# The twelve probability-times-value matmuls of a head pair, one after the other

## The chip, the cores and the metric

One core of one Trainium2 chip runs the whole program in one launch. The metric is device time in microseconds (us), from the first instruction to the last, the median of several runs. Engines are called as in the profile: PE is TensorE (matmuls; PEld its weight loads), DVE VectorE, ACT ScalarE, POOL GpSimd, SP the engine that issues most DMAs.

## The reference, cut to what matters

Two layers over 512 latent tokens and 256 context tokens, 1024 wide. Layer 0 mixes tokens by grouped-query attention, layer 1 by latent attention; each has 16 heads of 64. An MLP of 4096 follows each. What the change touches is the last line of the attention:

```python
s = jnp.einsum('bqhgd,bkhd->bhgqk', qi, k) * scale
p = jax.nn.softmax(s, axis=-1)
return jnp.einsum('bhgqk,bkhe->bqhge', p, v)
```

Latent queries see all 768 keys. Context queries (layer 0 only, since layer 1 needs no context output) see the 256 context keys.

## The kernel before, in words

Both attentions run through one class, `Attn`. Its `run` walks over items. An item is one head and 128 latent queries (or, in layer 0, one head and all 256 context queries). A head pair and 256 latent queries, a "half" below, is four items, so each layer has 8 pairs and 16 halves. Layer 0 has eight more, smaller groups for the context.

For an item PE makes the scores into a PSUM tile `big` (two of them): L867 and L868 in layer 0, L858 and L859 for its context queries, L1369, L1372 and L1373 in layer 1. DVE finds the maximum of each row (L713) and ACT the exponentials `prob` (L714). Two items later (`lag`) PE transposes the six blocks of `prob` (L729, into PSUM tiles `one`, of which there are four), and ACT (L736) and DVE (L738) copy them to `pT` in SBUF. When both heads and both query tiles of a half are there, `values` makes the steps that are left:

- `sums_of`: reciprocals of the row sums, and a broadcast of them (`rb`) on ACT
- six `block` steps, one for each 128 keys: two matmuls (L753), one for each head. Each has 64 output columns in the array: the first head's result goes to partitions 0 to 63 of the accumulator, the second head's to 64 to 127. Operands are float32
- `end`: two transposes of the broadcast sums (L762), a copy (L764) and the product that ends the half (L765)

`run` keeps these eight steps in a list `av` and takes two of them in each item, between that item's scores and its transposes. So one half's steps are spread over four items.

The code's order is not yet the order on an engine. When the program is built, a scheduler places the instructions of each engine by its own estimates of when inputs are ready, with buffers as limits. `tc.keep_in_program_order(x)` puts `x` behind the instruction that was recorded just before it on the same engine; the scheduler may still put others between the two. Loads of later weights (`early_weights`, `at`) and, in layer 0, the sums for the modulation vectors on POOL (`fill`: L204, L208, closed on PE by L215) hang on the count of items.

Of the kernel before, what the change touches and what calls it, by code (L numbers as in the profile page):

```python
# [19 lines left out]
P = 128  # L20
D = 1024
# [18 lines left out]
def backbone(ctx, tc, a, out):  # L40
    """Every float32 product runs as three float32r products: an operand is split exactly into
    hi = float32r(x) and lo = x - hi (12 significant bits each), and hi*hi, hi*lo and lo*hi are
    accumulated in PSUM."""
# [77 lines left out]
    def ada_bias(src, n, queue=nc.sync):  # L121
        """Row g of src [4, n] in rows 32 g and 32 g + 1."""
        ring = halves if n == P else brows
        ring.append(ring.pop(0))
        b = ring[-1]
        for g in range(4):
            queue.dma_start(b[32 * g : 32 * g + 2, 0:n], src[g : g + 1, :].to_broadcast([2, n]))
        return b[:, 0:n]
# [10 lines left out]
    def ada_finish(layer, v, half, n, o, bias):  # L139
        """o: PSUM [P, 512], the sums in rows 32 g + stream: to DRAM (gates) or transposed to SBUF."""  # L140
        w = D // n
        q = w // 4
        row = ada_row(o[:, 0:q], bias)
        if v % 3 == 2:
            for g in range(4):
                c0 = half * w + g * q
                nc.sync.dma_start(gates[2 * layer + v // 3, :, c0 : c0 + q], row[32 * g : 32 * g + 2, :])
            return
        tp = o[:, 256 : 256 + q]
        m = q // P  # L150
        for c in range(m):
            nc.tensor.transpose(tp[:, c * P : (c + 1) * P], row[:, c * P : (c + 1) * P], ident)
        if (layer, v) not in modT:
            modT[layer, v] = const.tile([P, KD, 2], F32, name=f"modT{layer}{v}")
        mv = modT[layer, v].rearrange("p (n g j) s -> p n j g s", n=n, g=4)
        for s in range(2):
            nc.vector.tensor_copy(
                out=mv[:, half, :, :, s], in_=tp.rearrange("p (c g r) -> p c g r", c=m, g=4)[:, :, :, s]
            )

    def ada_pe(layer, v, ts, bias):
        """Modulation vector v by TensorE alone: a list of steps."""
        o = []

        def step(k):
            if k == 0:
                o.append(one())
            for g in range(4):
                nc.tensor.matmul(
                    o[0][32 * g : 32 * g + 32, 0:256], scT[:, k, :], ts[k][:, g * 256 : g * 256 + 256],  # L170
                    start=(k == 0), stop=(k == KD - 1),
                )

        steps = [lambda k=k: step(k) for k in range(KD)]
        return steps + [lambda: ada_finish(layer, v, 0, 1, o[0], bias)]

    def ada_vec(layer, v, half, n, streams, pools, mult):
        """Part `half` of n of modulation vector v: silu(c)-weighted rows summed over the contraction
        tiles by GpSimd (or VectorE), over the partitions by TensorE. A list of steps to run; the last
        returns the step that ends it, for later. pools: tiles for the raw rows, the weighted rows and  # L180
        the sums."""
# [41 lines left out]
    class Fill:  # L223
        """Steps of side work; one that returns a further step has it run `lag` calls later."""
# [20 lines left out]
    def mod_ab(layer, sub, ln):  # L245
        """The per-feature scale and shift that take the normalized rows (before LayerNorm's gain
        and bias) to the modulated input of sublayer `sub`."""
        sh, sc = modT[layer, 3 * sub], modT[layer, 3 * sub + 1]
        A = const.tile([P, KD, 2], F32, name=f"modA{layer}{sub}")
        nc.vector.tensor_scalar_add(A, sc, 1.0)  # L250
        B = const.tile([P, KD, 2], F32, name=f"modB{layer}{sub}")
        nc.vector.tensor_tensor(
            out=B, in0=A, in1=lnbT[:, ln, :].unsqueeze(2).to_broadcast([P, KD, 2]), op=ALU.mult
        )
        nc.vector.tensor_tensor(out=B, in0=B, in1=sh, op=ALU.add)
        nc.vector.tensor_tensor(
            out=A, in0=A, in1=lngT[:, ln, :].unsqueeze(2).to_broadcast([P, KD, 2]), op=ALU.mult
        )
        return A, B

    def rsqrt(dst, src, n, scale):
        """dst = (src * scale + EPS) ** -0.5"""
        nc.vector.tensor_scalar(
            out=dst, in0=src, scalar1=scale, scalar2=EPS, op0=ALU.mult, op1=ALU.add
        )
        nc.gpsimd.tensor_tensor(out=dst, in0=dst, in1=nhalf[:, 0:n], op=ALU.pow)
# [7 lines left out]
    class LN:  # L274
        """LayerNorm of row tiles, the residual copy, and the modulated transpose of tile pairs."""
# [22 lines left out]
        def stats(self, z):  # L298
            """[1 / sigma, -mean / sigma] and the mean of the rows."""
# [19 lines left out]
        def gain(self, ln):  # L319
            """LayerNorm's gain and bias rows on every partition."""  # L320
            for nm in ("ln_g", "ln_b"):
                t = self.xp.tile([P, D], F32, name=nm)
                nc.sync.dma_start(t, a[nm][ln : ln + 1, :].to_broadcast([P, D]))
                self.gb[nm] = t
# [6 lines left out]
        def to_act(self, zs, col, s, A, B, aH, aL, temp, dve=(1,), pin=False):  # L331
            """Two normalized row tiles -> columns [col, col + 256) of the split activations; steps
            that return their last instructions."""
# [225 lines left out]
    def norm_a(src, n):  # L559
        """1 / rms of n heads of 64."""  # L560
# [11 lines left out]
    def norm_b(src, ss, n, t, i):  # L572
        """The normalized heads, or (latent tokens) the rotary terms: two summands."""
# [55 lines left out]
    def q_split(q, QS, lo, n):  # L629
        """Token tiles [lo, lo + n) of a head pair's q -> per head, the split transpose on two halves."""  # L630
# [48 lines left out]
    def early_weights(src, ws, n, i0, i1, step, at):  # L679
        """The first n weights of src: loads from item i0 of the attention on, splits from item i1 on."""  # L680
# [15 lines left out]
    class Attn:  # L696
        """Softmax attention over head pairs, in items of one head and 128 or (context) 256 queries.
        Of six transposed blocks ACT evacuates nact, DVE the others."""
# [5 lines left out]
        def softmax(self, S, ntile, width, sm):  # L704
            """S: PSUM [P, 2, 512], scores in [:, :, 0:width]; one row set over both banks, or
            (ntile 2) one in each. The exponentials; their row sums go to sm."""
# [16 lines left out]
        def transposed(self, pt, parts):  # L723
            """parts: (first block, PSUM evacuation to, by ACT or not); blocks of pt, transposed."""
# [15 lines left out]
        def values(self, PT, sums, v, kts, dst):  # L740
            """dst [P, 2, P]: both heads' outputs, transposed, over the row sums; a list of steps."""
# [8 lines left out]
            def block(n, kt):  # L750
                acc = env["acc"]
                for hh in range(2):
                    nc.tensor.matmul(  # L753
                        acc[64 * hh : 64 * hh + 64, 0:256], v(kt, hh), PT[hh][:, :, n, :],
                        start=(n == 0), stop=(n == len(kts) - 1),
                    )

# [12 lines left out]
            return [sums_of] + [lambda n=n, kt=kt: block(n, kt) for n, kt in enumerate(kts)] + [end]  # L770


        def run(self, first, prep, scores, vcol, o_of, npair, ctx_scores, fill, at):
            """first: the state of pair 0; prep(pair) -> (state, steps); scores(state, head, tile, S);
            vcol(kt, head); o_of(pair) -> destination; fill: further steps, one to an item; at: what
            to do at which item."""
# [10 lines left out]
            for i in range(len(items) + lag):  # L787
# [15 lines left out]
                av = av[2:]  # L803
                if i >= lag:
# [13 lines left out]
                    if h == 1 and (hf is None or q == 1):  # L818
# [5 lines left out]
                        )  # L824
                if steps:
                    steps.pop(0)()
# [69 lines left out]
    def out_proj(layer, wsrc, early, tiles, col0, o_of, x_src, x_dst, wxp, aH, aL, A, B, lnst, zst, x_ln):  # L896
        """y = attention output @ w_o, merged and normalized, tile by tile of 128 tokens. The rows
        of x still lack the gain and bias of LayerNorm x_ln, if any. Returns what is left to do for
        the last two tiles."""
# [53 lines left out]
    def mlp(layer, tiles, aH, aL, x_src, late, zst, lnst, fill, before_tail, finish):  # L953
        """Squared-ReLU MLP over the token tiles, G hidden tiles at a time; the last R groups are
        accumulated together, token tile by token tile. The rows of x still lack the gain and bias of
        the sublayer before's LayerNorm."""
# [122 lines left out]
        # With one stream its gate goes into the last weights' columns, else onto their products.  # L1079
# [57 lines left out]
    def low_rank(acc, n, sq, ss, cn, v, gT, dH, dL, col, late):  # L1137
        """RMS norm of a [P, 128 n] row tile; its gain and the split transpose are left to do."""
# [26 lines left out]
    def kv_tile(t):  # L1165
        """The latent rows and the rotary key of a tile."""
# [102 lines left out]
    def rope_keys(lo, n):  # L1269
        """The rotary key of token tiles [lo, lo + n), transposed, into every head's keys."""  # L1270
# [164 lines left out]
def _rope_tables(axis_dim):  # L1435
    """cos and signed sin of the 2-D rotary embedding, [P, 2, NLT, 2 * axis_dim]."""
# [12 lines left out]
def _layout(i):  # L1449
    f = {k: np.asarray(v) for k, v in i.items()}  # L1450

    def units(w, cols, per):
        """[K, *] columns `cols`, `per` contraction tiles side by side in each [P, per * cols]."""
# [63 lines left out]
```

## Time and profile before

| what | value |
|---|---|
| median of three runs | 1727.52 us (1726.24 to 1728.4) |
| span of the profiled execution | 1726.7 us |
| PE busy | 1670.8 us, 97% |
| DVE, ACT, POOL busy | 1125.1, 730.7 and 450.4 us |
| mean granted TensorE clock | 0.989 |
| first attention, first scores to last value matmul | about 137 to 358 us |
| second attention | about 1090 to 1293 us |

The profiled execution has no time of its own beside its span; the median of the three runs is 0.8 us above that span. "Busy" is time with at least one instruction of the engine running. PE's matmuls overlap each other, so an engine that is busy for the whole of a stretch can still do its work faster or slower. What is to be read is the distance from the start of one matmul to the start of the next.

### The profile page before, as it was taken

Reading aid. Unit: us, or ns where it says so; the run is one execution under the profiler, and the core shown is the slowest. Engines: PE = TensorE matmul, PEld = TensorE weight load, DVE = VectorE, ACT = ScalarE, POOL = GpSimd, SP = SyncE. Lnnn points to the kernel's source line nnn. Section 1 sums busy time; section 2 is a strip of 40 time slices with the busy share of each in tenths; the row PEclk is TensorE's granted clock in tenths of the full one; section 3 lists DMA queues with packets and bytes.
Section 4 is the critical chain, followed back from the end, with each engine's and each line's share of the span. In section 5 each row is a group of like instructions: output and inputs, shape, how many; then the busy total and the mean of one; then the engine's idle time right before and its main releaser. Section 6 shows DMA issues by size and latency. Waiting matters only on the chain.

```text
span 1726.7 us, 23376 instructions
## 1 busy us (share of the span) xinstructions
PE 1670.8 (97%) x9054; PEld 1377.1 (80%) x9054; DVE 1125.1 (65%) x1721; ACT 730.7 (42%) x1346; POOL 450.4 (26%) x317
## 2 busy tenths in 40 slices
PE   7998999999999999999999899999999899999996
PEld 5875777678988898889889798877778888888885
DVE  3688767756758676556547776656648745555578
ACT  2324666734544345233212256666654532222221
POOL 0157688300214154324013531000004200000034
PEclk9999999999999999999999999999999999999998
DMA  9412112132445256444212232000003532232222
GB/s 318 130 50 98 50 49 87 50 110 92 144 143 171 84 173 207 136 132 137 80 55 84 70 104 89 1 1 25 25 32 128 195 110 92 92 98 93 91 85 73
DMA packets 56384, 172.03 MB, mean 100 GB/s; under 512 B 7096, under 2 KB 10320, under 8 KB 56272
## 3 DMA queue, kind: packets, MB, share of 16 engines
q1 hardware_dynamic: 56240, 170.51, 29.6%
q8 instruction: 71, 1.16, 0.3%
q14 instruction: 41, 0.34, 0.1%
q10 hardware_dynamic: 32, 0.02, 0.0%
HBM read 161.03 MB, written 9.47 MB: 99 GB/s over the span
## 4 chain that ended last, share of the span: by engine, by line
PE 79%; DVE 11%; DMA 4%; ACT 2%; POOL 2%; issue 1%; SPq 0%; DVEq 0%; ACTq 0%; POOLq 0%
PE one L89 9%; PE one L91 9%; PE one L90 9%; PE one L753 8%; PE big L990 7%; PE big L994 7%; PE big L993 7%; PE one L729 5%; DVE wl L65 2%; PE one L930 2%; PE one L931 2%; PE one L934 2%; POOL xr L208 2%; DMA raw<-in_mlp_w_dram 2%; DMA sraw<-in_w_ada_dram 1%; PE big L1369 1%
## 5 line engine op out<-in xcount | busy, mean ns | idle before, releaser
L62 ACT CAST wh<-raw 128x1024 fp32r<-128x1024 f32 (+3 forms) x169 | 171.4, 1031 | 396.4 <-PE one L91 216.1
L65 DVE TENSOR_TENSOR wl<-raw,wh 128x1024 fp32r<-128x1024 f32 (+3 forms) x169 | 218.4, 1307 | 167.0 <-ACT wh L62 166.5
L990 PE MATMUL big<-actH,wh 128*128 128x384 f32 (+2 forms) x800 | 280.8, 352 | 3.2 <-ACT wh L62 3.2
L994 PE MATMUL big<-actH,wl 128*128 128x384 f32 (+2 forms) x800 | 279.6, 350 | 0.3 <-DVE wl L65 0.3
L993 PE MATMUL big<-actL,wh 128*128 128x384 f32 (+2 forms) x800 | 279.8, 350 | 0.0
L89 PE MATMUL one<-wh,hh 128*128 128x512 f32 x640 | 256.5, 402 | 12.4 <-ACT hh L62 7.3
L90 PE MATMUL one<-wl,hh 128*128 128x512 f32 x640 | 256.2, 400 | 1.3 <-DVE wl L65 1.3
L91 PE MATMUL one<-wh,hl 128*128 128x512 f32 x640 | 254.5, 399 | 2.7 <-DVE hl L65 2.7
L1072 DVE TENSOR_TENSOR yacc<-yacc,one 128x512 f32<-128x512 f32 x260 | 174.4, 683 | 110.7 <-PE one L91 110.1
L208 POOL TENSOR_TENSOR xr<-xr,raw 128x1024 f32<-128x1024 f32 x49 | 131.4, 2681 | 241.6 <-ACT raw L206 226.3
L990 PEld LDWEIGHTS big<-actH,wh 128*128 128x128 f32 x800 | 150.2, 188 | 16.6 <-ACT wh L62 4.1
L994 PEld LDWEIGHTS big<-actH,wl 128*128 128x128 f32 x800 | 150.3, 188 | 13.5 <-DVE wl L65 0.7
L993 PEld LDWEIGHTS big<-actL,wh 128*128 128x128 f32 x800 | 150.3, 188 | 12.3 <-issue 0.4
L89 PEld LDWEIGHTS one<-wh,hh 128*128 128x128 f32 x640 | 122.2, 191 | 43.6 <-ACT hh L62 8.4
L713 DVE TENSOR_REDUCE nm<-big 128x1 f32<-128x768 f32 x128 | 122.1, 954 | 46.7 <-PE big L1373 29.6
L91 PEld LDWEIGHTS one<-wh,hl 128*128 128x128 f32 x640 | 121.7, 190 | 33.0 <-DVE hl L65 4.1
L90 PEld LDWEIGHTS one<-wl,hh 128*128 128x128 f32 x640 | 122.2, 191 | 27.6 <-DVE wl L65 1.7
L328 POOL TENSOR_TENSOR xr<-xr,ln_g 128x1024 f32<-128x1024 f32 x14 | 37.2, 2661 | 401.6 <-DMA xr<-xres 394.6
L714 ACT ACTIVATE prob<-big,nm 128x768 f32<-128x768 f32 x128 | 116.0, 906 | 37.4 <-DVE nm L713 34.4
L729 PE MATMUL one<-ident,prob 128*128 128x128 f32 x832 | 126.6, 279 | 3.2 <-DVE QS L65 3.1
L753 PE MATMUL one<-pT,V 128*64 128x256 f32 x768 | 129.6, 391 | 0.0
L729 PEld LDWEIGHTS one<-ident,prob 128*128 128x128 f32 x832 | 96.4, 141 | 33.4 <-issue 20.9
(247 smaller groups left out, 2883.9 us busy)
## 6 DMA issues: line engine op xcount, KB each, us to landing
raw<-in_mlp_w_dram SPq DMA_DIRECT2D x128, 512.0 KB
raw<-in_w_ada_dram SPq DMA_DIRECT2D x56, 512.0 KB
sraw<-in_w_ada_dram SPq DMA_DIRECT2D x32, 256.0 KB
araw<-in_w_ada_dram SPq DMA_DIRECT2D x32, 256.0 KB
raw<-in_w_o_dram SPq DMA_DIRECT2D x16, 512.0 KB
xr<-xres SPq DMA_DIRECT2D x14, 512.0 KB
raw<-in_w_qkv_dram SPq DMA_DIRECT2D x12, 512.0 KB
xres<-z SPq DMA_DIRECT2D x10, 512.0 KB
```

Source lines behind the costliest of these rows:

```text
L62: return nc.scalar.copy(out=dst, in_=src)
L65: return nc.vector.tensor_tensor(out=dst, in0=src, in1=hi.bitcast(F32), op=ALU.subtract)
L89: nc.tensor.matmul(o, lh, rh, start=start, stop=False)
L90: nc.tensor.matmul(o, lh, rl, start=False, stop=False)
L91: nc.tensor.matmul(o, ll, rh, start=False, stop=stop)
L208: nc.gpsimd.tensor_tensor(out=accs[s], in0=accs[s], in1=dst, op=ALU.add)
L729: nc.tensor.transpose(tp[:, j * P : (j + 1) * P], pt[:, (lo + j) * P : (lo + j + 1) * P], ident)
L753: nc.tensor.matmul(acc[64 * hh : 64 * hh + 64, 0:256], v(kt, hh), PT[hh][:, :, n, :], start=(n == 0), stop=(n == len(kts) - 1),)
L990: mm = nc.tensor.matmul(o, wh[:, ks], aH[:, k, s:e], start=(k == 0), stop=False)
L993: nc.tensor.matmul(o, wh[:, ks], aL[:, k, s:e], start=False, stop=False)
L994: nc.tensor.matmul(o, wl[:, ks], aH[:, k, s:e], start=False, stop=(k == KD - 1))
L1072: nc.vector.tensor_tensor(out=yacc[i][:, cs], in0=yacc[i][:, cs], in1=accs[hf], op=ALU.add)
```

## The change

The six `block` steps become one step `blocks`, which records all twelve value matmuls; every one but the first is kept in program order behind the one before it. The list `av` now has three steps. In the item after the half is complete `run` takes `sums_of` and `blocks` between that item's scores and its transposes, and then `end`, which is taken out as `late`, behind the transposes. For the context queries of layer 0 `blocks` records four matmuls. Comments and docstrings were also taken out; lines behind L765 of the old file move by up to seven.

```diff
             def block(n, kt):
                 acc = env["acc"]
                 for hh in range(2):
-                    nc.tensor.matmul(
+                    mm = nc.tensor.matmul(
                         acc[64 * hh : 64 * hh + 64, 0:256], v(kt, hh), PT[hh][:, :, n, :],
                         start=(n == 0), stop=(n == len(kts) - 1),
                     )
+                    if n or hh:
+                        tc.keep_in_program_order(mm)
...
-            return [sums_of] + [lambda n=n, kt=kt: block(n, kt) for n, kt in enumerate(kts)] + [end]
-
+            def blocks():
+                for n, kt in enumerate(kts):
+                    block(n, kt)
+
+            return [sums_of, blocks, end]
...
                 for f in av[:2]:
                     f()
-                av = av[2:]
+                late, av = av[2:3], av[3:]
...
+                for f in late:
+                    f()
                 if steps:
                     steps.pop(0)()
```

What the scheduler makes of it, on PE, at two places. The first is in layer 0, the half that follows a context group: L729 are transposes of probabilities, L753 value matmuls, L867 and L868 scores (L874 and L875 after the change). Before, the second half of that piece of the program reads:

```order
L729 MATMUL one<-ident,prob 128x128 x2
L753 MATMUL one<-pT,V_95 64x256 x3
L729 MATMUL one<-ident,prob 128x128 x4
L753 MATMUL one<-pT,V_95 64x256
L867 MATMUL big<-KL,QS 128x384
L868 MATMUL big<-KH,QS 128x384
L867 MATMUL big<-KL,QS 128x384
L868 MATMUL big<-KH,QS 128x384
L729 MATMUL one<-ident,prob 128x128 x2
L753 MATMUL one<-pT,V_95 64x256 x5
L729 MATMUL one<-ident,prob 128x128 x4
L753 MATMUL one<-pT,V_95 64x256
```

Ahead of these rows stand two more L753 of the same half, each alone, so that the twelve come in six groups of 1, 1, 3, 1, 5 and 1. The same half after the change, whole:

```order
L729 MATMUL one<-ident,prob 128x128 x6
L753 MATMUL one<-pT,V_95 64x256
L874 MATMUL big<-KL,QS 128x384
L875 MATMUL big<-KH,QS 128x384
L874 MATMUL big<-KL,QS 128x384
L875 MATMUL big<-KH,QS 128x384
L753 MATMUL one<-pT,V_95 64x256 x4
L729 MATMUL one<-ident,prob 128x128 x6
L753 MATMUL one<-pT,V_95 64x256 x7
```

The twelve now come in three groups, of 1, 4 and 7: the first is not tied to what stands before it, and the scheduler has put six transposes between two that are tied.

The second place is in layer 1, PE, a half whose value matmuls stand between the scores of the next items (L1372 and L1373 are two of the three score lines, and L762 the transposes of the sums). Before:

```order
L753 MATMUL one<-pT,V_9447 64x256 x2
L729 MATMUL one<-ident,prob 128x128 x4
L753 MATMUL one<-pT,V_9447 64x256 x7
L1369 MATMUL big<-KPH_9448,QL 128x384 x2
L1372 MATMUL big<-KPL_9449,QH 128x384
L1373 MATMUL big<-KPH_9448,QH 128x384
L1372 MATMUL big<-KPL_9449,QH 128x384
L1373 MATMUL big<-KPH_9448,QH 128x384
L753 MATMUL one<-pT,V_9447 64x256 x3
L762 MATMUL one<-ident,rb 128x128 x2
```

After, the corresponding half (score lines are L1376, L1379 and L1380 now, and the sums' transposes L764):

```order
L1376 MATMUL big<-KPH_9448,QL 128x384 x2
L1379 MATMUL big<-KPL_9449,QH 128x384
L1380 MATMUL big<-KPH_9448,QH 128x384
L1379 MATMUL big<-KPL_9449,QH 128x384
L1380 MATMUL big<-KPH_9448,QH 128x384
L753 MATMUL one<-pT,V_9447 64x256 x12
L729 MATMUL one<-ident,prob 128x128 x6
L764 MATMUL one<-ident,rb 128x128 x2
```

Here all twelve stand together, behind a full set of scores. Outside the two attentions PE's order is the same in both programs; on SP two loads `araw` and on POOL one product `atmp` move by one place.

## Rows read from the trace of the kernel before

**Rows 1.** The page: PE's busy time; the chain that ended last, by engine

```profile
PE 1670.8 (97%) x9054; PEld 1377.1 (80%) x9054; DVE 1125.1 (65%) x1721; ACT 730.7 (42%) x1346; POOL 450.4 (26%) x317
...
PE 79%; DVE 11%; DMA 4%; ACT 2%; POOL 2%; issue 1%; SPq 0%; DVEq 0%; ACTq 0%; POOLq 0%
```

**Rows 2.** Two windows: length, busy us by PE, PEld, DVE, ACT, POOL; clock; DMA

```profile
200.00:250.00 50.00, 50.00 (x338) 35.33 (x336) 35.85 (x59) 32.77 (x85) 36.18 (x33) 1.00 0.13 43
...
1150.00:1200.00 50.00, 50.00 (x323) 38.33 (x321) 31.24 (x52) 32.89 (x68) 0.00 (x0) 1.00 0.06 22
```

**Rows 3.** Line L753: duration ns min/median/max, first and last start

```profile
L753 PEld LDWEIGHTS one<-pT,V x768: 132/137/137, 165.3 to 1292.5; 128*64 128x64 f32 x192
L753 PE MATMUL one<-pT,V x768: 379/379/431, 165.3 to 1292.7; 128*64 128x256 f32 x192
```

**Rows 4.** Timeline of PE, layer 0: start us, us until its last end, records

```profile
191.97 0.65 PE L753 MATMUL one<-pT,V 128*64 128x256 f32 x2
192.55 0.44 PE L729 MATMUL one<-ident,prob 128*128 128x128 f32 x2
192.91 1.08 PE L753 MATMUL one<-pT,V 128*64 128x256 f32 x6
193.92 0.66 PE L729 MATMUL one<-ident,prob 128*128 128x128 f32 x4
194.51 0.65 PE L753 MATMUL one<-pT,V 128*64 128x256 f32 x2
195.08 0.44 PE L867 MATMUL big<-KL,QS 128*128 128x384 f32 x1
195.36 0.33 PE L868 MATMUL big<-KH,QS 128*128 128x384 f32 x1
...
195.89 0.38 PE L729 MATMUL one<-ident,prob 128*128 128x128 f32 x2
```

**Rows 5.** Timeline of PE, layer 0: transposes and scores with no L753 near

```profile
183.32 1.47 PE L729 MATMUL one<-ident,prob 128*128 128x128 f32 x12
184.55 0.42 PE L867 MATMUL big<-KL,QS 128*128 128x384 f32 x1
184.81 0.34 PE L868 MATMUL big<-KH,QS 128*128 128x384 f32 x1
184.99 0.33 PE L867 MATMUL big<-KL,QS 128*128 128x384 f32 x1
```

**Rows 6.** The chain in order of time: start us, us to the next piece

```profile
354.15 1.01 PE one L753 x8
...
1105.14 2.31 PE one L753 x20
...
1195.85 0.58 PE one L753 x4
1196.43 0.59 PE one L729 x4
1197.02 1.87 PE one L753 x14
```

**Rows 7.** Groups by line, 150 to 340 us: xcount, busy us, mean ns, idle before

```profile
L713 DVE TENSOR_REDUCE nm<-big 128x1 f32<-128x768 f32 x58 | 55.2, 951 | 14.5 <-PE big L868 14.1
L714 ACT ACTIVATE prob<-big,nm 128x768 f32<-128x768 f32 x58 | 52.4, 904 | 14.9 <-DVE nm L713 14.2
...
L738 DVE COPY pT<-one 128x512 f32<-128x512 f32 x58 | 39.4, 680 | 11.6 <-PE one L729 11.4
...
L736 ACT COPY pT<-one 128x256 f32<-128x256 f32 x56 | 20.8, 371 | 29.2 <-PE one L729 28.7
```

**Rows 8.** Groups by line, 1100 to 1290 us

```profile
L736 ACT COPY pT<-one 128x512 f32<-128x512 f32 x62 | 36.6, 590 | 31.5 <-PE one L729 31.1
L738 DVE COPY pT<-one 128x256 f32<-128x256 f32 x61 | 25.5, 419 | 27.2 <-PE one L729 26.4
```

**Rows 9.** Waits, 150 to 340 us: us in total, times, longest

```profile
PE big L867 <- ACT prob L714: 1.3, 2, 0.9
```

**Rows 10.** Timeline of POOL and of PE: end of a modulation sum, and its use

```profile
188.48 1.28 POOL L208 TENSOR_TENSOR aacc<-aacc,araw 128x512 f32<-128x512 f32 x1
...
208.70 0.66 PE L215 MATMUL one<-aacc,onehot 128*32 128x128 f32 x16
```

## What I expect, and how it follows

> **What bounds the kernel now.** I read the page first: PE is busy for 97% of the span and makes 79% of the chain that ended last [rows 1]. So the time of a stage is PE's time unless a stage shows otherwise. The windows of the two attentions show no otherwise: in 50 us of each, PE is busy for all 50.00, DVE and ACT for 31 to 36 [rows 2]. "Busy for all 50" hides the question, though. In the timeline the reader should look at distances from start to start. There PE is not equally quick at the same work.
>
> Take the value matmuls. One of them is two records of the trace (768 records of layer 0's and layer 1's latent halves [rows 3] are 384 matmuls in the program). A group of one (x2) lasts 0.57 or 0.58 us until the next kind of instruction starts, a group of three (x6) 1.01 us [rows 4]. A group of two (x4) also lasts 0.58, one of four (x8) 1.01, one of seven (x14) 1.87, one of ten (x20) 2.31 [rows 6]. All lie on one line: 0.145 us for the group, and 0.432 us for each step, where a step holds two matmuls, or one if it is the odd one. The two heads of a key block use different columns of the array and run side by side; a matmul that is cut off from its partner takes a whole step alone.
>
> The neighbours pay too. Twelve transposes and the first score matmul behind them last from 183.32 to 184.81, a score matmul alone 0.18 (184.81 to 184.99), so a transpose takes (1.49 - 0.18) / 12 = 0.109 us [rows 5]. Four transposes between two groups of value matmuls take 0.59 (193.92 to 194.51, and again in layer 1 [rows 6]) instead of 0.44: 0.15 us more for one way out of a group and one way into the next. Where scores follow, the first takes 0.28 instead of 0.18 [rows 4].
>
> So each group, apart from its steps, costs 0.145 + 0.15 = 0.295 us of PE's time, in which PE counts as busy.
>
> **The change part by part.** First, fewer groups. Counted over the whole order of both programs, the 416 value matmuls stand in 135 groups before and in 85 after (layer 0: 77 to 52; layer 1: 58 to 33). That is 50 groups fewer. Not all become twelve: of the 32 halves 12 come whole and the others in two to four pieces, mostly 1, 4 and 7 or 1, 8 and 3. 50 x 0.295 = 14.8 us. If scores rather than transposes stood at every way out, the price would be about 0.05 more for each, 17 us in all; I take 14.8, since transposes are the commoner neighbour.
>
> Second, fewer steps. With the odd ones counted as whole steps, there are 265 before and 237 after (148 to 131, and 117 to 106). 28 x 0.432 = 12.1 us.
>
> Third, what may come back as waits. The work of a half is the same, but PE now does it unevenly: items with scores and transposes alone, then one with the whole group. What is late next? (a) The copies to `pT`. Between the last transposes and the value matmuls the order still has a set of scores, as before: in layer 0 four score matmuls, 0.81 us (195.08 to 195.89 [rows 4]); in layer 1 six, 6 x 0.18 = 1.08. The copy needs 0.37 us on ACT in layer 0 and 0.59 in layer 1 [rows 7, 8], plus whatever ACT is doing, at worst one exponential of 0.90 [rows 7]. So the wait is nothing at best, and at worst 0.90 + 0.37 - 0.81 = 0.46 us in a half of layer 0 and 0.90 + 0.59 - 1.08 = 0.41 in one of layer 1: 14 us over 32 halves. DVE's blocks are used two steps or more later and need less. (b) The scores, which wait until the exponentials of two items ago have left their PSUM tile. Today that costs 1.3 us in 190 [rows 9]. In layer 0 an item without value matmuls takes PE 4 x 0.18 + 6 x 0.109 = 1.4 us, but DVE 0.95 + 0.68 = 1.63 [rows 7]: it falls behind by 0.25 an item, for three items 0.75, and catches up under the group. In layer 1 DVE's copy is shorter, 0.42 [rows 8], and with the same maximum it needs 1.37 against PE's 1.08 + 0.65 = 1.7: it keeps up. Two tiles for scores and the lag of two items give it more room than 0.75 us. So I put (a) and (b) together at 2 us, three or four waits like those of today; the ends are 0 and 14 + 16 x 0.75 = 26.
>
> Fourth, the rest is free. `sums_of` and `end` have the same instructions; `end` comes two items earlier and gives one of four `one` tiles back earlier, which can only help. The two loads and one product that move by one place on SP and POOL lie within POOL's sums, which have slack: the first is complete at 188.48 + 1.28 = 189.8 and PE needs it at 208.70 [rows 10], 19 us later. PE gets ahead by at most 25 x 0.295 + 17 x 0.432 = 14.7 us in all of layer 0's attention. Behind the attentions PE's order is unchanged and PE bound, so time won stays won.
>
> Sum: 1726.7 - 14.8 - 12.1 + 2 = 1701.8 of span; the median of the runs stands 0.8 above the profiled span: **1702.6 us**, 24.9 us less (1.4%). With the 2 us shared evenly, 13.7 fall in layer 0 and 11.1 in layer 1 (25 x 0.295 + 11 x 0.432 - 1).
>
> The granted clock is 1.00 in both windows [rows 2], which is the upper of its two levels, and PE leaves no gap there; all prices are from rows at that level, and I expect the level to stay.
>
> One thing speaks for less. A weight load takes 0.132 to 0.137 us [rows 3], close to the 0.145 us that a group pays ahead of its steps. If each matmul in a group had to show its own load, joining groups would save no load, only the neighbours' 0.15 and the steps: 50 x 0.15 + 12.1 - 2 = 17.6 us instead of 24.9. But the steps of 0.432 us are the same in groups of four, seven and ten [rows 6], so I take it that the loads inside a group lie under the matmul before. The Trainium skill, "TensorE: Matmul & The Clock Gate", Part 3, The mechanism, states that a weight load overlaps matmuls in flight only where its row group differs; all value matmuls use all 128 rows, so by that rule the smaller gain would come. The trace does not agree with it.
>
> **The rivals.**
>
> Waits take a part (1711 to 1724): (a) and (b) cost not 2 but 10 to 23 us, each running near its worst. For it: DVE's 0.25 us an item in layer 0. Against: the order keeps the scores ahead of the group, and PE's waits are near zero today. 0.08.
>
> Loads show inside groups, as costed above: 1727.5 - 17.6 = 1709.9. Against it stand the equal steps. 0.04.
>
> The group is a wall, slower than before: nothing for DVE is queued while PE does the whole group, so that DVE's work and the group add up instead of overlapping. A half of layer 0 takes 13.1 us today (58 latent items in 190 us [rows 7], four to a half), and DVE is busy for 72% of it [rows 2], 9.4 us. Behind a wall it would take 9.4 + 2.74 (the group: 0.145 + 6 x 0.432) + 0.81 (scores) + 0.90 (the exponential that the next copies wait for) = 13.9 us, 0.8 more; layer 0 would lose 13 us. In layer 1 the same sum is 12.3 (62 items) x 0.62 + 2.74 + 1.08 + 0.90 = 12.3, no change. The end is 1740. It decides from the point where a half waits for more than 26.9 / 32 = 0.84 us. Against: scores stand ahead of the group in both excerpts, so there is a maximum and an exponential to do under it. 0.04.
>
> The change doesn't do what it says, because the scheduler breaks the groups up. It partly does, and that is counted above; only if waits took all the rest would it end within 0.2% of before: 0.04.
>
> More gain (below 1697): fewer groups also free score tiles earlier, and the few waits of today go. 0.05.
>
> **How the numbers follow.** The forecast, 1697 to 1710, has 0.75; with the rivals that makes 1. A measurement of this kernel can tell about 0.2%, 3.5 us, from no change. Faster by more than that: 0.75 + 0.08 + 0.04 + 0.05 = 0.92; within: 0.04; slower: 0.04. The range of 8 in 10 is 1697 to 1712: the forecast, the loads' case and the near end of the waits.
>
> **What would show it.** Right: in the timeline of the changed kernel a group of twelve (x24) lasts 2.74 us until the next start; the number of groups of L753 falls by 50; PE's waits for ACT and DVE in the attentions grow by no more than 2 or 3 us; the first attention is shorter by 13 to 14 us, the second by 11, and everything between and behind keeps its length. Wrong: steps inside a long group over 0.44 us (the loads), or, in the view of waits, PE at L874 or L1376 waiting for ACT's exponentials, or at L753 for the copies, by more than 0.3 us in a half (waits); or the attentions shorter and an MLP longer (given back later).

## The result, and the profile after

The changed kernel takes 1703.01 us (median of four runs, 1702.17 to 1704.88), the kernel before 1727.28 in four runs on the same chip. The ratio is 0.9857, with a 95% interval of 0.9843 to 0.987: 24.3 us less. Forecast were 1702.6 us and 24.9 less. The profiled execution's span is 1703.1 us, at the same mean granted clock of 0.989.

The page of the changed kernel, its busy times and its chain by engine, answers to [rows 1]:

```profile
PE 1645.4 (97%) x9054; PEld 1377.4 (81%) x9054; DVE 1118.4 (66%) x1721; ACT 730.4 (43%) x1346; POOL 450.3 (26%) x317
...
PE 77%; DVE 10%; POOL 5%; DMA 4%; ACT 3%; issue 2%; SPq 0%; DVEq 0%; POOLq 0%; ACTq 0%
```

PE has the same 9054 records and is busy for 25.4 us less, of a span that is 23.6 us shorter. The same matmuls take less time; no gap was closed.

Two windows of the changed kernel (columns as in [rows 2]):

```profile
200.00:250.00 50.00, 50.00 (x376) 38.46 (x376) 38.14 (x65) 36.20 (x96) 38.33 (x36) 1.00 0.15 48
...
1150.00:1200.00 50.00, 49.52 (x345) 41.41 (x345) 33.79 (x57) 35.96 (x74) 0.00 (x0) 1.00 0.09 33
```

The clock stands at 1.00 as before. PE is busy for 50.00 and 49.52 of the 50 us, with 376 records in place of 338 in the first window and 345 in place of 323 in the second.

The timeline of PE in layer 0 shows a half whose twelve matmuls come as 1, 4 and 7, as in the order that the section on the change prints (only that two of the six transposes stand ahead of the four here), and the whole group that follows (columns as in [rows 4]):

```profile
189.13 0.65 PE L753 MATMUL one<-pT,V 128*64 128x256 f32 x2
189.70 0.44 PE L874 MATMUL big<-KL,QS 128*128 128x384 f32 x1
...
190.50 0.38 PE L729 MATMUL one<-ident,prob 128*128 128x128 f32 x2
190.81 1.08 PE L753 MATMUL one<-pT,V 128*64 128x256 f32 x8
191.83 0.66 PE L729 MATMUL one<-ident,prob 128*128 128x128 f32 x4
192.41 1.94 PE L753 MATMUL one<-pT,V 128*64 128x256 f32 x14
194.29 0.44 PE L764 MATMUL one<-ident,rb 128*128 128x128 f32 x2
...
199.73 0.28 PE L866 MATMUL big<-KH,QS 128*128 128x256 f32 x1
199.94 2.88 PE L753 MATMUL one<-pT,V 128*64 128x256 f32 x24
202.75 0.44 PE L729 MATMUL one<-ident,prob 128*128 128x128 f32 x2
```

The groups of four and of seven last as before, 1.02 and 1.88 us from start to start [rows 6]. The four transposes between them still take 0.58. This x24 has 2.81 us to the next start; the median of the twelve such groups in the trace is 2.74, as forecast. In layer 1 they stand in the chain of the changed kernel one after the other (start, us to the next piece):

```profile
1105.83 2.74 PE one L753 x24
1108.57 0.81 PE one L729 x6
...
1154.73 2.74 PE one L753 x24
1157.48 0.81 PE one L729 x6
```

Counted over the whole trace, L753 stands in 85 groups (12 of them x24); before it were 135, 61 of them a single matmul.

Where the time came from, in us between starts on PE (read from both timelines):

| stretch | before | after | difference |
|---|---|---|---|
| first attention, first scores to last value matmul | 220.70 | 208.80 | -11.90 |
| from there to the second attention's first scores | 732.61 | 733.82 | +1.2 |
| second attention | 202.86 | 190.92 | -11.94 |
| from there to the end | 433.93 | 432.98 | -0.95 |

The two stretches outside the attentions have the same order on PE. Other runs below have 731.9 to 741.1 us for the first of them, so +1.2 is scatter. In the longest (cut at six, below) the granted clock averages 0.72 from 350 to 362 us, where it is 1.00 in the changed kernel.

PE's waits inside the attentions, from the view of PE's waits of the changed kernel, 136 to 360 us and, last row, 1075 to 1295 us (us in total, times, longest):

```profile
PE one L753 <- DVE pC L738: 3.9, 1, 3.9
PE one L729 <- DVE QS L65: 3.1, 2, 2.9
PE one L729 <- DVE pT L738: 1.2, 1, 1.2
PE big L874 <- ACT prob L714: 0.9, 1, 0.9
PE one L729 <- ACT prob L714: 0.9, 1, 0.9
...
PE one L729 <- ACT prob L718: 0.5, 1, 0.5
...
PE big L1376 <- ACT prob L714: 0.5, 1, 0.5
```

The first two of these rows are waits for DVE's early work of layer 0, and stand in the kernel before with 4.0 and 3.1 us. In layer 0 the waits for exponentials (`prob`) were 1.3 us [rows 9] and are 2.3 now (0.9, 0.9 and 0.5); one of 0.9 comes at 340 us, where all scores of the attention are made and PE stands before the last item's transposes. Layer 1 has 0.5 us of them, before none. New, too, are the 1.2 us, which have a cause in the timeline of the changed kernel (DVE and PE; the bracket is idle time before):

```profile
298.61 1.62 DVE L65 TENSOR_TENSOR wl<-raw,wh 128x1024 fp32r<-128x1024 f32 x1 [0.51 <-ACT wh L62]
300.26 0.69 DVE L716 TENSOR_REDUCE nm<-big 128x2 f32<-128x512 f32 x1
300.86 0.68 DVE L738 COPY pT<-one 128x512 f32<-128x512 f32 x1
301.60 1.09 PE L729 MATMUL one<-ident,prob 128*128 128x128 f32 x8 [1.22 <-DVE pT L738]
```

DVE splits an early weight for 1.62 us. Behind it stand a maximum and the copy that gives a `one` tile back, and PE's next transposes need that tile.

### The profile page after: what moved, and what is told of

The parts are those of the page before. It is cut to its first block, busy times and chain, and to the rows that moved or that the text cites. A ratio compares the mean times of both kernels' runs of the same rounds, so it can differ in the third digit from the quotient of the medians.

```text
span 1703.1 us, 23372 instructions
## 1 busy us (share of the span) xinstructions
PE 1645.4 (97%) x9054; PEld 1377.4 (81%) x9054; DVE 1118.4 (66%) x1721; ACT 730.4 (43%) x1346; POOL 450.3 (26%) x317
## 4 chain that ended last, share of the span: by engine, by line
PE 77%; DVE 10%; POOL 5%; DMA 4%; ACT 3%; issue 2%; SPq 0%; DVEq 0%; POOLq 0%; ACTq 0%
PE one L89 10%; PE one L91 9%; PE one L90 9%; PE big L997 7%; PE big L1000 7%; PE big L1001 7%; PE one L753 5%; PE one L729 4%; DMA araw<-in_w_ada_dram 2%; PE one L937 2%; PE one L941 2%; PE one L938 2%; DVE wl L65 2%; POOL xr L208 1%; PE big L1376 1%
## 5 line engine op out<-in xcount | busy, mean ns | idle before, releaser
L729 PE MATMUL one<-ident,prob 128*128 128x128 f32 x832 | 122.0, 277 | 5.8 <-DVE QS L65 3.1
L729 PEld LDWEIGHTS one<-ident,prob 128*128 128x128 f32 x832 | 96.7, 141 | 28.1 <-issue 16.8
L753 PE MATMUL one<-pT,V 128*64 128x256 f32 x768 | 107.7, 387 | 0.0
```

Source lines behind the costliest of these rows:

```text
L729: nc.tensor.transpose(tp[:, j * P : (j + 1) * P], pt[:, (lo + j) * P : (lo + j + 1) * P], ident)
L753: mm = nc.tensor.matmul(acc[64 * hh : 64 * hh + 64, 0:256], v(kt, hh), PT[hh][:, :, n, :], start=(n == 0), stop=(n == len(kts) - 1),)
```

## The experiments

All ran beside the kernel before, whose medians were 1727.4, 1728.5, 1728.6 and 1729.2 us in the four sets. "A wait" below is time of PE, from start to start, above what the same rows take elsewhere by [rows 3 to 6]: 15.7 us in layer 0 and 1.3 in layer 1 before, 17.9 and 2.1 after (summed over all of PE's records in an attention). That is more than the view of waits lists, which counts only time without any matmul running. It also holds what PE loses at the lower level of its clock: from 145 to 170 us the granted clock averages 0.86 in both kernels. Medians of different sets are compared as they are; the kernel before differs by up to 1.9 us between the sets.

**What does it, the pins or the new place?** The changed program built without `keep_in_program_order` has, on every engine, the same instructions in the same order with the same waits: the pins do nothing there. The opposite is pins with the old place of the steps:

```diff
-            return [sums_of, blocks, end]
+            return [sums_of] + [lambda n=n, kt=kt: block(n, kt) for n, kt in enumerate(kts)] + [end]
...
-                late, av = av[2:3], av[3:]
+                late, av = [], av[2:]
```

> Each value matmul kept in program order behind the last PE instruction recorded before it, but the steps in their old places, two to an item: 161 groups and 264 steps against 135 and 265 before. Theory: 26 x 0.295 - 0.4 = 7.3 us more than before, 1734 to 1737 with waits. Rival (freeing earlier is what counts): nothing is freed earlier and the work is the same, so no change from before, 1727.

It took 1734.44 us (1733.27 to 1735.32), ratio 1.0039 (1.0026 to 1.0052): 7.0 us slower than before. So the pins carry none of the gain, and alone they make more groups and cost time. The gain comes from recording the twelve matmuls in one step. `end`, which comes earlier besides, was not moved alone; the full-width kernel below, which has it too, gains nothing.

**One layer at a time.** `joined` chooses the new or the old steps for each `Attn`.

```diff
-            return [sums_of, blocks, end]
+            if not self.joined:
+                return [sums_of] + [lambda n=n, kt=kt: block(n, kt) for n, kt in enumerate(kts)] + [end]
+            return [sums_of, blocks, end]
...
-                late, av = av[2:3], av[3:]
+                late, av = (av[2:3], av[3:]) if self.joined else ([], av[2:])
```

> The change in layer 0 alone: 77 to 52 groups, 148 to 131 steps there. Theory: 14.7 us of PE's work less; the changed kernel's trace has its first attention 11.9 us shorter and 1.2 us given back behind it, so 1715 to 1717. If the two layers' gains hang on each other, it lies elsewhere.

> The change in layer 1 alone: 58 to 33 groups, 117 to 106 steps there. Theory: 12.1 us of PE's work less; 1714.5 to 1716. The gains of the two layers alone add up to that of both, 24.3 us, within 1.

Layer 0 alone: 1717.25 us, just above the 1717 expected, ratio 0.9939 (0.9924 to 0.9954), 10.2 less; its attention takes 209.33 us, the other is unchanged at 202.86. Layer 1 alone: 1715.26, ratio 0.9928 (0.991 to 0.9945), 12.2 less; its attention takes 190.95. Together 22.3 of the 24.3 us; within 1 was expected, and the 2.0 that are missing are within the intervals. Each layer keeps its gain by itself.

**Only whole groups.** PE takes the attentions in the order in which the code records them, so that the scheduler breaks nothing up: 40 groups and 208 steps.

```diff
-    att.run(
+    with tc.manual_schedule(engines={nc.tensor.engine}):
+      att.run(
... (and the same around layer 1's `att.run`)
```

> PE's order in both attentions is the order of the code, so that every group is whole: 40 groups and 208 steps against 85 and 237 of the changed kernel. If the price is 0.295 us for a group and 0.432 for a step (theory), PE's work falls by another 45 x 0.295 + 29 x 0.432 = 25.8 us: 1677 us, plus what PE now waits because nothing can be put in between; I expect 3 to 15 us of waits, 1680 to 1692. If a group costs nothing beyond its steps (rival: the change won by freeing the accumulator and pT earlier), only the steps count, 12.5 us less at best, and the waits on top: 1691 or more, most likely above 1703.

It took 1698.23 us (1696.0 to 1699.39), ratio 0.9831 (0.9814 to 0.9847). That is 4.8 less than the changed kernel and above the 1680 to 1692 expected. The work did fall: 45 groups and 29 steps fewer are 13.3 + 12.5 = 25.8 us by the prediction's prices. Layer 1 kept most of its part (184.29 us, 6.6 less than after; waits 4.7). Layer 0 did not (205.16, only 3.6 less): its waits rose from 17.9 to 32.5 us. The view of waits of this kernel, 140 to 345 us:

```profile
PE big L874 <- ACT prob L718: 5.3, 5, 2.4
PE big L874 <- ACT prob L714: 4.3, 7, 3.0
...
PE one L729 <- DVE QS L65: 3.3, 1, 3.3
...
PE one L152 <- DVE modrow L132: 2.0, 2, 1.4
```

The scores wait for exponentials for 9.6 us where the changed kernel waits for 0.9. This is the prediction's (b). It comes when PE may not take other work in between. The granted clock is lower here from 145 to 170 us, 0.73 against 0.86 in the changed kernel, but that explains little: in the kernel with layer 1 alone changed it is 0.73 there too, and its first attention takes 220.94 us against 220.70 before.

**The price of a group and of a step, each by itself.** Both kernels cut the twelve in two, with a set of transposes between, under the same strict order: after six (one group more in a half, no step more), or after five (5 and 7: a group and a step more).

```diff
+            cut = 6 if len(kts) == 6 else 4
+            return [sums_of, lambda: blocks(0, cut), lambda: (blocks(cut, 2 * len(kts)), end())]
... (the second kernel has 5 in place of the first 6; `blocks(lo, hi)` records matmuls lo to hi - 1)
```

> PE in the order of the code, as in the run with whole groups, but the item's transposes recorded between the sixth and the seventh value matmul: 70 groups and 208 steps. It differs from the run with whole groups by 30 groups alone. Theory: 30 x 0.295 = 8.9 us more than that run. Rival (a group costs nothing beyond its steps): the same time within 2 us, or less, since the later six wait less for their copies.

> The same with the cut between the fifth and the seventh: groups of 5 and 7 instead of 6 and 6, so the two heads of one key block are parted. 70 groups and 238 steps. Theory: 30 x 0.432 = 13.0 us more than with the cut after six. Rival (a parted matmul costs nothing, the work is the same): no difference.

Cut at six: 1707.26 us (1704.37 to 1712.16), ratio 0.9873 (0.9857 to 0.989), 9.0 more than whole groups; 30 x 0.295 is 8.9. So close a match is luck: the runs of this kernel spread over 7.8 us, and measured against the kernel before in its own set the step is 7.9. In the profiled runs layer 0 gives 6.9 us for its 15 groups, with a granted clock of 0.93 from 300 to 325 us where whole groups have 1.00. Layer 1, with few waits, gives 3.9 us for 15 groups, 0.26 each. Cut at five: 1717.14 (1713.98 to 1719.31), ratio 0.9935 (0.992 to 0.9949), 9.9 more again; 13.0 was expected. Layer 1 gives 6.1 us for 15 steps, 0.41 each; in layer 0 it is 2.4 only, against a run that had the lower clock just named, and where PE waits anyway. The timeline of the second in layer 1 shows the prices:

```profile
1159.46 1.51 PE L775 MATMUL one<-pT,V 128*64 128x256 f32 x10
1160.90 0.88 PE L729 MATMUL one<-ident,prob 128*128 128x128 f32 x6
1161.70 1.94 PE L775 MATMUL one<-pT,V 128*64 128x256 f32 x14
1163.57 0.44 PE L764 MATMUL one<-ident,rb 128*128 128x128 f32 x2
```

Five matmuls take 1.44 us and seven 1.87, 3.31 together; the twelve in one group take 2.74. A group's 0.145 and one step's 0.432 make the difference. The transposes between take 0.80 instead of 6 x 0.109 = 0.65, the neighbours' 0.15.

**Is it the break, or the half array?** Here each value matmul uses all 128 columns. The first kernel is made from the kernel before, the second from the changed one; the scheduler's order differs from theirs in places (155 and 76 groups in place of 135 and 85).

```diff
-                        acc[64 * hh : 64 * hh + 64, 0:256], v(kt, hh), PT[hh][:, :, n, :],
-                        start=(n == 0), stop=(n == len(kts) - 1),
+                        acc[:, 0:256], v(kt, hh), PT[hh][:, :, n, :],
+                        start=(n == 0 and hh == 0), stop=(n == len(kts) - 1 and hh == 1),
... (and 128 columns of V in place of 64, in both calls of `att.run`)
```

> The kernel before with value matmuls 128 columns wide instead of 64: both heads' 64 value columns are loaded (in layer 0 two key heads' columns) and both heads of a pair are added into one accumulator over all 128 partitions, so the attention's values are not the reference's; number of matmuls, their moving columns, buffers and other engines' work stay. 155 groups and 416 steps, since no two matmuls can run side by side. Theory (the 0.295 us is the way into and out of the half-width form, so full-width groups are free): 151 steps more at 0.432 = +65 us, 135 x 0.295 = 40 us less: 1752. Rival (any change between value matmuls and others costs 0.295): +65 + 6 = 1798.

> The changed kernel with the same full-width value matmuls and the same part left wrong (both heads of a pair added into one accumulator): 76 groups, 416 steps. Theory: groups are free, so the same as the full-width kernel with the steps in their old places, within 3 us. Rival (any change of kind costs 0.295, or freeing buffers earlier is what won): 79 x 0.295 = 23 us less than that.

The first took 1753.7 us (1751.78 to 1756.66), ratio 1.0149 (1.0134 to 1.0164), as expected from 416 single steps with no price on a group. The second took 1757.46 (1756.26 to 1759.38), ratio 1.017 (1.0155 to 1.0186): it has 76 groups instead of 155 and is 3.8 us slower, where 0.295 a group would have saved 23; within 3 us was expected. The timeline of PE in the first:

```profile
192.38 0.60 PE L753 MATMUL one<-pT,V 128*128 128x256 f32 x2
192.63 0.53 PE L867 MATMUL big<-KL,QS 128*128 128x384 f32 x1
192.99 0.34 PE L868 MATMUL big<-KH,QS 128*128 128x384 f32 x1
...
193.51 0.38 PE L729 MATMUL one<-ident,prob 128*128 128x128 f32 x2
193.73 0.60 PE L753 MATMUL one<-pT,V 128*128 128x256 f32 x2
194.16 0.60 PE L729 MATMUL one<-ident,prob 128*128 128x128 f32 x4
194.60 3.19 PE L753 MATMUL one<-pT,V 128*128 128x256 f32 x14
```

A group of one takes 0.43 us here (193.73 to 194.16), not 0.58, and four transposes behind it 0.44, not 0.59. Where a score follows, it starts earlier and lasts longer; the two together take 0.61 us (192.38 to 192.99), a step of 0.43 and a score of 0.18, where the kernel before takes 0.85 (194.51 to 195.36 [rows 4]). Both parts of the price are gone, though the groups are broken as before. The loads are even longer, by this kernel's source line:

```profile
L753 PEld LDWEIGHTS one<-pT,V x768: 186/190/192, 165.8 to 1318.0; 128*128 128x128 f32 x192
L753 PE MATMUL one<-pT,V x768: 377/379/483, 165.9 to 1318.2; 128*128 128x256 f32 x192
```

A load of 0.190 us shows nowhere. So the price belongs to the passage between matmuls of 64 columns and of 128. What happens at it, the loads show (timeline of PEld: start, us, records; in brackets the idle time before). First the kernel before, whose matmuls [rows 4] start at 192.91, 193.92 and 194.51:

```profile
192.91 0.62 PEld L753 LDWEIGHTS one<-pT,V 128*64 128x64 f32 x6 [0.17 <-issue]
193.92 0.42 PEld L729 LDWEIGHTS one<-ident,prob 128*128 128x128 f32 x4 [0.39 <-issue]
194.51 0.19 PEld L753 LDWEIGHTS one<-pT,V 128*64 128x64 f32 x2 [0.17 <-issue]
```

Then the full-width kernel, whose matmuls above start at 193.73, 194.16 and 194.60:

```profile
193.62 0.30 PEld L753 LDWEIGHTS one<-pT,V 128*128 128x128 f32 x2
193.95 0.58 PEld L729 LDWEIGHTS one<-ident,prob 128*128 128x128 f32 x4
194.49 2.89 PEld L753 LDWEIGHTS one<-pT,V 128*128 128x128 f32 x14
```

At full width the first load starts 0.11 or 0.21 us ahead of its matmul, under the one before. At a change of width it starts together with its matmul, into a group and out of it. So the first load is not hidden there. Each of the two passages of a group costs about 0.147 us (half of 0.295), close to one load (0.132 to 0.137 us). Whether PE spends that time on the load or on something else that the load waits for, no run parts.

With that price gone, the new place costs 3.8 us, most of it waits, as far as the views show (3.1 us): by the second kernel's view of waits, PE's transposes at L729 wait for exponentials for 1.4 us in layer 0 and 0.8 in layer 1, and the scores of layer 1 for 0.9, all of which the first has not.

**Do the two heads run side by side?** The changed kernel, but with all matmuls of one head ahead of all of the other.

```diff
-                for n, kt in enumerate(kts):
-                    block(n, kt)
+                acc = env["acc"]
+                for hh in range(2):
+                    for n, kt in enumerate(kts):
+                        mm = nc.tensor.matmul(
...
```

> The changed kernel with the first head's matmuls of a half recorded ahead of the second head's, so that neighbours use the same columns and cannot run side by side: 79 groups, 400 steps. Theory: 163 x 0.432 - 6 x 0.295 = 69 us more than the changed kernel, 1772; some of it hides waits. Rival (only the number of matmuls counts): 1701 to 1703.

It took 1768.95 us (1768.43 to 1771.41), ratio 1.0237 (1.0222 to 1.0252), 66 more than the changed kernel with fewer groups (79). Its timeline in layer 1:

```profile
1158.74 2.80 PE L776 MATMUL one<-pT,V 128*64 128x256 f32 x12
1161.47 0.44 PE L729 MATMUL one<-ident,prob 128*128 128x128 f32 x2
...
1170.35 4.59 PE L776 MATMUL one<-pT,V 128*64 128x256 f32 x24
1174.87 0.33 PE L729 MATMUL one<-ident,prob 128*128 128x128 f32 x1
```

Six matmuls of one head take 2.73 us, 0.145 + 6 x 0.432, where six of two heads take 1.45 (the median in the kernel cut at six). The twelve of two heads, one head behind the other, take 4.52 instead of 2.74. By the prices that is 10 steps, where the expectation counted 11: at the change of heads two matmuls of each still meet. That is the step.

**Six and six in layer 0.** An attempt to get whole groups' work without layer 0's waits: six matmuls in the item after the half is complete and six two items later, in strict order; layer 1 whole.

```diff
-    att = Attn(st_att, 4, 2, "right")
+    att = Attn(st_att, 4, 2, "right", (6, 0, 12))
... (matmuls recorded up to the sixth, none, up to the twelfth; layer 1 has (12,))
```

> PE in the order of the code in both attentions; whole groups of twelve in layer 1, and in layer 0 six matmuls in the item after a half is complete and six two items later: 55 groups and 208 steps. In the run with whole groups layer 1 was 18.6 us shorter than before with 21.5 us of work less, layer 0 only 15.5 us shorter with 61 steps' and groups' worth of 31 us less, with PE waiting for the exponentials. Theory: 15 groups more cost 4.4 us in layer 0 and give most of these waits, some 12 us, back: 1684 to 1692. Rival (the waits come from the fixed order itself, wherever the matmuls stand): 1698 + 4.4 = 1702 or more.

It took 1698.76 us (1696.25 to 1700.49), ratio 0.9822 (0.9808 to 0.9837), and missed what was expected; it lies between the theory and the rival, and within the interval of whole groups. Waits in layer 0 are 27.5 us, 5 less than with whole groups, and the 15 groups more cost 15 x 0.295 = 4.4. The longest waits are still of scores for exponentials (L881 is this kernel's line for them), 130 to 355 us:

```profile
PE big L881 <- ACT prob L715: 4.4, 3, 3.6
```

So spreading the groups in this way does not free layer 0; PE waits in both fixed orders.

**A faster version.** The scheduler's order in layer 0, a strict one in layer 1 alone; then, besides, layer 0's transposes issued only behind the last value matmul of the group before them.

```diff
+    with tc.manual_schedule(engines={nc.tensor.engine}):
+      att.run(first1, prep1, scores1, lambda kt, h: V1[:, kt, h * 64 : h * 64 + 64], o_of1, 8, None, None, at)
```

> Layer 0 as in the changed kernel, layer 1 with PE in the order of the code: 68 groups and 227 steps. Theory: layer 1's attention as in the run with whole groups, 6.6 us shorter than in the changed kernel (its work falls by 17 x 0.295 + 10 x 0.432 = 9.3 us): 1696 to 1697. If whole groups don't pay in layer 1 alone, 1703.

```diff
+                hold = ExitStack()
+                if late and self.nact == 2:
+                    hold.enter_context(tc.issue_after(self.last.ins))
```

> As the run before, and in layer 0 the scheduler stays free but may not place the item's transposes ahead of the last value matmul: 37 groups and 124 steps there against 52 and 131. Theory: 15 x 0.295 + 7 x 0.432 = 7.4 us less work in layer 0, of which waits take back some: 1689 to 1696. Rival (layer 0 is bound by its waits for the exponentials, whichever way the groups are joined): no better than the run before, 1696 or more.

The first took 1696.99 us (1695.37 to 1698.51), ratio 0.9818 (0.9802 to 0.9833), as expected. The second took 1695.47 (1694.46 to 1696.96), ratio 0.9811 (0.9797 to 0.9826). It is the fastest here and beats both kernels, but its gain on the first, 1.5 us, is within the intervals, so the rival is not ruled out. The 7.4 us of work that it saves in layer 0 (15 groups x 0.295 and 7 steps x 0.432) come back in good part as waits, 22.4 us against 18.3.

## Why the prediction was right, step by step

**Fewer groups, 14.8 us: right.** The trace has 85 groups after 135. The price was measured by itself: cutting 30 groups in two cost 9.0 us against 8.9, with the spread named above, and 0.26 us each in the layer with few waits. It is the price of changing between 64 and 128 columns, since at full width it vanishes. The Trainium skill, "TensorEngine Tiling (Array Packing)", Key Properties, states that a change of the tiling mode drains the engine. The runs agree that a change costs time, 0.295 us for the way in and out; a drain no row shows, only that the first load does not start ahead.

**Fewer steps, 12.1 us: right.** One step more in 15 halves cost 0.41 us each, and without partners the groups took 4.52 us instead of 2.74. The Trainium skill states in the same section that different tiles can load and multiply in parallel; the trace agrees, with 0.432 us for two matmuls side by side as for one.

**The loads: right that they lie under the matmul before, inside a group.** A whole group lasts 2.74 us, and at full width a load of 0.190 us shows nowhere. A group's first load does not lie under one, as the loads above show; the prediction had its time in the 0.145 us. The sentence of the Trainium skill on which the prediction's rival rests ("TensorE: Matmul & The Clock Gate", Part 3, The mechanism) ties the overlap to different row groups; here every matmul uses all 128 rows, and by that sentence 1709.9 us would have come. The measurement decides against it for this kernel. The Trainium skill names in the same section also a background weight buffer as a target of early loads; the loads inside a group agree with that, though the buffer itself no row shows.

**Waits, 2 us: 3.0 measured, and unevenly.** Summed over all of PE's records at the prices of before, the work fell by 14.1 us in layer 0 and 12.8 in layer 1, together the 26.9 of the sum (counted groups and steps alone give 14.7 and 12.1). Above that, layer 0 waits for 2.2 us more and layer 1 for 0.8. 26.9 - 3.0 = 23.9 is what the two attentions lost (11.90 + 11.94). So layer 0's part was put too high (13.7) and layer 1's too low (11.1); that the total came within 1 us is in part luck, since the two errors offset each other. In layer 0 the waits are of two kinds: 1.0 us more for exponentials, the prediction's (b), and 1.2 us that were not costed, DVE's split of an early weight ahead of a maximum and a copy. Of (a), copies for the value matmuls, nothing came. The wait for the context's copies of 3.9 us stands where it stood, at 161 us; what PE wins ahead of it in layer 0 it waits away there.

**POOL's sums and the rest: right.** PE took the first sum at 204.94 us, and it was complete at 189.0 (timelines of POOL and PE); the slack of 19 us [rows 10] became 16. POOL's 5% in the new chain is no wait of PE's: the chain enters POOL by a load of `araw` that ends at 300.27 us, as a releaser of the maximum at 300.26 in the rows above, and DVE was busy with its split until 298.61 + 1.62 = 300.23 anyway. The clock stayed at 1.00 in both windows, and its mean at 0.989.

**The rivals.** The wall did not come: by the view of PE's waits PE has none at L753 for its copies in either attention, beyond the one for the context. Strict whole groups are the nearest to the wall, with 32.5 us of waits in layer 0, and even they gain. That waits take a part is real, but small as long as the scheduler may put other work between; with the order fixed it took 14.6 us in layer 0 (32.5 - 17.9).

That the work was worth its price in full holds for both layers; why a fixed order makes only layer 0 wait was argued in the prediction from DVE's 1.63 us in an item against PE's 1.4. No run changed DVE's share, so this stays open.

## What to carry to other kernels

A busy engine can still be paying: compare the distance between starts for the same instruction in groups of different length, and a line through them gives the price of a group and of a step. Keep matmuls of half the columns together and in pairs that use opposite halves, away from full-width transposes and scores. Forbidding the scheduler every break pays only where the other engines keep up; here it did in layer 1 and mostly not in layer 0.

## What was not expected of the hardware

A passage between matmuls of 64 and of 128 columns costs 0.295 us there and back, and the same break at full width costs nothing that a timeline shows (0.431 us for one matmul, 0.109 for each transpose beside it). A matmul of 64 columns without a partner takes as long as one of 128 (0.432 us). Loads of 0.137 and of 0.190 us are hidden alike inside a group; the first load behind a change of width starts only with its own matmul (192.91 and 193.92 us in the kernel before), where without a change it starts 0.11 or 0.21 us ahead.
